# Two transformer-like layers on one core: hi and lo activations as one 512-column moving side in the wide products

## The chip, the cores and the metric

One core of a Trainium2 chip runs the whole program. The metric is device time in microseconds (us) of one execution, as the median of the runs; lower is better. Five engines work side by side, each through its own queue and in a fixed order: TensorE (PE, with its weight loads shown apart as PEld), VectorE (DVE), ScalarE (ACT), GpSimd (POOL) and SyncE (SP, which here only issues DMAs). TensorE writes to PSUM, which has eight banks of 512 f32 columns for each of 128 partitions.

## The reference

256 tokens of width 1024 pass through two layers, all in f32. Cut to what matters here:

```
first layer:   xn = rms_norm(x, norm1_g);  proj = xn @ w_in
               ... three small attentions on q, k, v -> o_nsa
               u = conv_c * conv_x;  y = 3-tap causal conv of u;  z = conv_b * y
               mixed = sigmoid(gate_a) * (o_nsa @ w_branch_a) + sigmoid(gate_b) * (z @ w_branch_b)
               x = x + mixed @ w_out
               x = x + square(relu(rms_norm(x) @ w_up)) @ w_down        # 1024 -> 4096 -> 1024
second layer:  a 31-tap convolution branch, an attention with top-k selection, two gates, their product with w_mix_out,
               cross attention to 256 memory rows (k, v = rms_norm(mem) @ wkv)
               h = h + square(relu(rms_norm(h) @ w_ff1)) @ w_ff2;  rms_norm(h)
```

conv_b, conv_c, conv_x, gate_a and gate_b are column ranges of proj, each 1024 wide.

## The kernel before

Activations are kept transposed: features on the 128 partitions, 256 tokens along the free side (T = 256). A weight matrix comes from HBM in units of 1 MB (`wr`, 128 x 2048: four blocks of 128 input features by 512 output features). Since f32 products are wanted from f32r passes, every number is split in two: ACT writes a rounded copy (`wh`, L123, two halves of 128x1024), DVE the rest (`wl`, L126, two halves). Activations are split in the same way into `hi` and `lo`. `Stream` loads and splits ahead: at the start of a unit it has the unit two further on split, and since there are three `wh`/`wl` buffers, that split has to wait until PE has left the unit just finished. So at every unit's start ACT's next `wh` half waits for PE.

A product of 128 input by 128 output features is `mm3` (L260 to L268): three matmuls of 256 moving columns into the same 256 PSUM columns, `wh` by hi (L264), `wh` by lo (L266) and `wl` by hi (L268). `Feat` is a group: 512 output features, so four such column ranges, in two PSUM tiles `m` of one bank each (a pool `psm` of four banks, so two groups have place at a time). A group takes `len(kts) // 4` units; most take two, the down products of the feed-forward eight. In its last unit a group goes through output features 0 and 1 first (called b = 0 below) and gives that tile to its eviction function while PE goes on with features 2 and 3 (b = 1). The eviction reads the PSUM tile itself: for instance `cs = ps * rb` (L802), `cs = ps * cs` (L805), `y = ps * y` (L820), `d = ps * rb` (L832), or `relu(ps)` on ACT (L929) followed by a square on DVE (L930) and the split into `hh` (L396 on ACT, L397 on DVE).

Between halves of a unit `pump()` runs one step of side work: the steps of the first layer's attentions, the statistics of the norms, the 31-tap convolution, the second attention. An attention step of the first layer has a few PE matmuls (scores L743 to L745, transposes L769, products L779 and L785), and on DVE a masked score (L747), a maximum (L750), reciprocals and scalings (L751 to L758). Ahead of these steps come two that go through POOL: `coqk` (L629 on DVE, L631 a power on POOL, L633 and on again on DVE) and `msc` (L688, L689 on POOL, `kcb` L694 on DVE).

PE's instructions keep the order in which they are written. ACT's and DVE's are ordered when the program is built, by a planner that knows priorities (side steps are urgent) and estimated times; on the chip each engine keeps that order, so an instruction that waits holds up all that stand behind it on its engine.

The order of the groups in the first layer: q, k, a token product (`Tok`), then for each half of the conv features (hf 0 and 1) conv_c, conv_x, conv_b; gate_a twice (`ta`), gate_b twice (`tb`), z by w_branch_b twice (`zs`), the attention branch, w_out, eight groups of w_up (the first two taken unit by unit in turn), two groups of w_down. Then the memory keys (`km`), and the second layer, whose feed-forward up product has eight groups again; its down product is a `Tok` product with 512 moving columns (L355 to L357).

Of the kernel before, what the change touches and what calls it, by code (L numbers as in the profile page):

```python
# [16 lines left out]
T = 256  # L17
# [38 lines left out]
class Split:  # L56
# [12 lines left out]
    def lo(self, k, n=1):  # L69
        return self._part(1, k, n)  # L70

    def _part(self, h, k, n):
# [88 lines left out]
def hybrid_conformer_kernel(ctx, tc, stop, dbg, xT, memT, wall, wtok, wkiwi, wcmp, par_d, cst_d, gfin_d, out):  # L161
# [5 lines left out]
    sm = ctx.enter_context(tc.tile_pool(name="sm", bufs=2))  # L167
    psm = ctx.enter_context(tc.tile_pool(name="psm", bufs=4, space=bass.MemoryType.PSUM))
    pss = ctx.enter_context(tc.tile_pool(name="pss", bufs=3, space=bass.MemoryType.PSUM))
# [22 lines left out]
    def PS(name="s"):  # L192
        return pss.tile([128, 512], F32, name=name, tag="s")

    def bc(ap, n):
# [19 lines left out]
    def v4(ap):  # L215
        return ap.rearrange("p n (s a) -> p n s a", s=2)
# [41 lines left out]
    ALL8 = list(range(8))  # L258

    def mm3(ps_ap, wh, wl, xh, xl, first, last, part=None):  # L260
        ps_ap = ps_ap.rearrange("p (a s) -> p a s", s=2)
        xh, xl = turns(xh), turns(xl)
        if part in (None, 0):
            P.matmul(out=ps_ap, lhsT=wh, rhs=xh, start=first, stop=False, skip_group_check=True)  # L264
        if part in (None, 1):
            P.matmul(out=ps_ap, lhsT=wh, rhs=xl, start=False, stop=False, skip_group_check=True)  # L266
        if part in (None, 2):
            P.matmul(out=ps_ap, lhsT=wl, rhs=xh, start=False, stop=last, skip_group_check=True)  # L268

    class Feat:  # L270


        def __init__(self, act, kts, evac, kmajor=False):
            self.act, self.kts, self.evac, self.kmajor = act, kts, evac, kmajor
            self.nch = len(kts) // 4
            self.ps = None

        def chunk(self, c):
            if self.ps is None:
                self.ps = [psm.tile([128, 2, T], F32, name="m", tag="m") for _ in range(2)]  # L280
            ps, act = self.ps, self.act
# [38 lines left out]
    class Tok:  # L320
# [10 lines left out]
        def chunks(self, c, num, mid=None):  # L331

            if self.ps is None:
                self.ps = [psm.tile([128, 512], F32, name="m", tag="m") for _ in range(2)]
            ps, act, n = self.ps, self.act, self.n
# [39 lines left out]
    def prod(gs, pair=False):  # L375
        if pair:
            for c in range(gs[0].nch):
                for g in gs:
                    g.chunk(c)
        else:  # L380
            for g in gs:
                for c in range(g.nch):
                    g.chunk(c)

    def group(act, kts, evac, kmajor=False):
        prod([Feat(act, kts, evac, kmajor)])

# [95 lines left out]
    with tc.manual_schedule(engines=MANUAL):  # L483
# [3 lines left out]
        with tc.manual_schedule(engines={mybir.EngineType.Activation}):  # L487
            nc.scalar.dma_start(out=par0, in_=par_d[:, 0:8])
            A.activation(out=S([128, 1], "tab"), in_=ones[:, 0:1], func=AF.Exp)
        warm = psm.tile([128, 2, T], F32, name="m", tag="m")  # L490
        for i in range(WARM):
# [306 lines left out]
        for hf in range(2):  # L798
# [23 lines left out]

            group(xs, ALL8, ev_c)
            group(xs, ALL8, ev_x)
            group(xs, ALL8, ev_b)

        ta, tb = B8(name="ta"), B8(name="tb")
        for dst in (ta, tb):
            for hf in range(2):
                def ev_g(ps, o, n):  # L830
                    d = dst[hf][:, o:o + n]
                    V.tensor_tensor(v4(d), ps, v4(bc(c1["rb"], n)), op=ALU.mult)  # L832
                    A.activation(out=d, in_=d, func=AF.Tanh, scale=0.5)

                group(xs, ALL8, ev_g)


        m1 = B8(name="m1")
        for hf in range(2):
            def ev_bb(ps, o, n):  # L840
                gated(m1[hf][:, o:o + n], tb[hf][:, o:o + n], ps)

            group(zs, ALL8, ev_bb)
        drain(at1)
# [12 lines left out]

        def residual(act, kts, x, sp, gname, scale_b=None, kmajor=False, pair=True, stats=None):

            def one(hf):  # L860
# [28 lines left out]

                return Feat(act, kts, ev, kmajor=kmajor and hf == 0)  # L890

# [6 lines left out]
        def ffn_up(act, src, tagr, bcast):  # L898
# [25 lines left out]
            for g in range(8):  # L924
                hs.tiles += HL("hh", 4).tiles

                def ev(ps, o, n, g=g):
                    r = S([128, 2, T], "pr", PR_BUFS)
                    A.activation(out=v4(r), in_=ps, func=AF.Relu)  # L929
                    V.tensor_tensor(r, r, r, op=ALU.mult)  # L930
                    split_into(hs, r, n, 4 * g + o)

                gs.append(Feat(act, ALL8, ev))
            prod(gs[:2], pair=True)
# [44 lines left out]
        st3 = {}  # L979
        residual(hs, list(range(32)), x, None, None, scale_b=res["b"], pair=False, stats=st3)  # L980
        drain(msd)
# [31 lines left out]

        group(mems, ALL8, ev_km)
        drain(n3)
# [13 lines left out]
        def heads_pv(pt, nb, v, h0, sp, tt, pool=None):  # L1029

            if pool is psm:
                po = psm.tile([128, 2, T], F32, name="m", tag="m").rearrange("p a t -> p (a t)")
            else:
                po = PS() if pool is pss else pso.tile([128, 512], F32, name="o", tag="o")
# [163 lines left out]
        for hf in range(2):  # L1198
# [21 lines left out]
            kiwi = S([128, T], "rb", 4)  # L1220
            ps = psm.tile([128, 2, T], F32, name="m", tag="m")
            wh, wl = W.next()
# [302 lines left out]
```

## Time and profile before

| | |
|---|---|
| runs, median (lowest to highest) | 895.32 us (895.29 to 895.41), 3 runs |
| profiled execution, its own time | 895.22 us |
| its span, first to last instruction | 893.4 us |
| PE busy | 881.9 us (99%), 7240 matmuls |
| DVE busy | 659.8 us (74%) |
| ACT busy | 545.4 us (61%) |
| POOL busy | 18.6 us (2%) |

Times inside the execution are microseconds from the span's start. A row of the timeline gives start, duration, engine, line, operation, out<-in, and in brackets the idle time of the engine before it and what ended that. Matmuls overlap in the pipeline, so the distance from one matmul's start to the next is what it costs, not its duration; DVE and ACT instructions overlap by about 0.1 us with the next.

### The profile page before, as it was taken

The numbers are of one execution on the slowest core, as the hardware profiler recorded it, in microseconds if no ns is written. First come the engines' busy times: TensorE is split into PE (matmuls) and PEld (weight loads), VectorE is DVE, ScalarE is ACT, GpSimd is POOL, SyncE is SP. The second block draws the span as 40 slices with busy tenths as digits, with TensorE's granted clock in tenths as the row PEclk, the third lists the DMA queues.
The fourth block names the chain that finished last, engine by engine and source line by source line (L and its number), as shares of the span: only waits on it lengthen the run. The fifth ranks groups of instructions, "written<-read, shape, count | busy, mean of one in ns | idle before, by whom it ended". The sixth has DMA issues, their size and how long they took to land.

```text
span 893.4 us, 17269 instructions
## 1 busy us (share of the span) xinstructions
PE 881.9 (99%) x7240; PEld 852.8 (95%) x7240; DVE 659.8 (74%) x1037; ACT 545.4 (61%) x925; POOL 18.6 (2%) x21
## 2 busy tenths in 40 slices
PE   9999999999999999999999999999999999999996
PEld 8999999999999999999998989999999999998885
DVE  6678899457787675648699999997787777665542
ACT  7634667444575564434697799977566657554432
POOL 0121000000000000000000000000000000000000
PEclk9999999999999999999999999999999999999999
DMA  8944623455555566554553356354565265555531
GB/s 305 313 161 146 222 98 140 158 211 198 190 190 189 192 241 219 197 189 140 186 209 107 139 193 236 112 192 166 199 250 203 104 216 189 190 202 209 198 142 48
DMA packets 25566, 165.01 MB, mean 185 GB/s; under 512 B 2960, under 2 KB 3600, under 8 KB 6928
## 3 DMA queue, kind: packets, MB, share of 16 engines
q1 hardware_dynamic: 25056, 163.37, 51.8%
q8 instruction: 57, 0.93, 0.4%
q10 hardware_dynamic: 432, 0.53, 0.2%
q14 instruction: 21, 0.17, 0.1%
HBM read 162.58 MB, written 1.05 MB: 183 GB/s over the span
## 4 chain that ended last, share of the span: by engine, by line
PE 89%; DVE 5%; ACT 2%; issue 1%; DMA 1%; POOL 1%; POOLq 0%; DVEq 0%
PE m L264 23%; PE m L266 23%; PE m L268 23%; PE m L355 4%; PE m L356 4%; PE m L357 4%; DVE wl L126 2%; PE m L295 2%; DMA wr<-in_wall_dram 1%; PE m L352 1%; DVE y L1147 1%; PE o L785 1%; PE s L769 1%; PE s L1065 1%; POOL coqk L631 1%
## 5 line engine op out<-in xcount | busy, mean ns | idle before, releaser
L126 DVE TENSOR_TENSOR wl<-wr,wh 128x1024 fp32r<-128x1024 f32 (+2 forms) x300 | 350.4, 1191 | 155.2 <-ACT wh L123 154.8
L123 ACT ACTIVATE wh<-wr 128x1024 fp32r<-128x1024 f32 (+2 forms) x300 | 298.5, 1028 | 204.2 <-PE m L266 95.9
L264 PE MATMUL m<-xnh,wh 128*128 128x256 f32 x376 | 106.6, 283 | 0.0
L266 PE MATMUL m<-xnh,wh 128*128 128x256 f32 x376 | 103.4, 275 | 0.0
L268 PE MATMUL m<-xnh,wl 128*128 128x256 f32 x376 | 103.4, 275 | 0.0
L264 PE MATMUL m<-xh,wh 128*128 128x256 f32 x384 | 100.5, 282 | 0.9 <-ACT xh L523 0.9
L266 PE MATMUL m<-xh,wh 128*128 128x256 f32 x384 | 98.0, 276 | 0.0
L268 PE MATMUL m<-xh,wl 128*128 128x256 f32 x384 | 97.8, 275 | 0.0
L1146 ACT ACTIVATE cp<-u,par 128x255 f32<-128x255 f32 (+23 forms) x192 | 78.8, 492 | 0.0
L266 PEld LDWEIGHTS m<-xnh,wh 128*128 128x128 f32 x376 | 72.2, 192 | 0.7 <-issue 0.5
L264 PEld LDWEIGHTS m<-xnh,wh 128*128 128x128 f32 x376 | 72.2, 192 | 0.7 <-issue 0.5
L264 PEld LDWEIGHTS m<-xh,wh 128*128 128x128 f32 x384 | 69.8, 192 | 2.8 <-issue 1.4
L268 PEld LDWEIGHTS m<-xnh,wl 128*128 128x128 f32 x376 | 72.2, 192 | 0.0
L264 PE MATMUL m<-x5h,wh 128*128 128x256 f32 x256 | 70.8, 277 | 0.0
L264 PE MATMUL m<-fh,wh 128*128 128x256 f32 x256 | 70.6, 276 | 0.0
L264 PE MATMUL m<-hh,wh 128*128 128x256 f32 x256 | 70.6, 276 | 0.0
L268 PE MATMUL m<-x5h,wl 128*128 128x256 f32 x256 | 70.4, 275 | 0.0
L266 PE MATMUL m<-fh,wh 128*128 128x256 f32 x256 | 70.4, 275 | 0.0
L268 PE MATMUL m<-fh,wl 128*128 128x256 f32 x256 | 70.4, 275 | 0.0
L266 PE MATMUL m<-hh,wh 128*128 128x256 f32 x256 | 70.4, 275 | 0.0
L268 PE MATMUL m<-hh,wl 128*128 128x256 f32 x256 | 70.4, 275 | 0.0
L266 PE MATMUL m<-x5h,wh 128*128 128x256 f32 x256 | 70.4, 275 | 0.0
(380 smaller groups left out, 2318.1 us busy)
## 6 DMA issues: line engine op xcount, KB each, us to landing
wr<-in_wall_dram SPq DMA_DIRECT2D x145, 1024.0 KB, 4.9
wr<-in_wall_dram SPq DMA_DIRECT2D x4, 512.0 KB, 9.1
mem<-in_memT_dram SPq DMA_DIRECT2D x4, 512.0 KB, 5.8
wr<-in_wtok_dram SPq DMA_DIRECT2D x2, 560.0 KB, 5.5
wr<-in_wall_dram SPq DMA_DIRECT2D x4, 256.0 KB, 5.1
wck<-in_wcmp_dram SPq DMA_DIRECT2D x2, 512.0 KB, 8.6
cst<-in_cst_dram SPq DMA_DIRECT2D x1, 776.0 KB, 10.7
x<-in_xT_dram SPq DMA_DIRECT2D x2, 256.0 KB, 4.2
```

The source lines that it names most:

```text
L123: self.nc.scalar.activation(out=hi[:, sl], in_=raw[:, sl], func=AF.Copy)
L126: self.nc.vector.tensor_sub(lo[:, sl], raw[:, sl], hi[:, sl].bitcast(F32))
L264: P.matmul(out=ps_ap, lhsT=wh, rhs=xh, start=first, stop=False, skip_group_check=True)
L266: P.matmul(out=ps_ap, lhsT=wh, rhs=xl, start=False, stop=False, skip_group_check=True)
L268: P.matmul(out=ps_ap, lhsT=wl, rhs=xh, start=False, stop=last, skip_group_check=True)
L295: P.matmul(out=plain(ps[o // 2])[:, o % 2], lhsT=wh[:, kk, sl], rhs=v3(act.raw(k)), start=first, stop=last, skip_group_check=True)
L352: P.matmul(out=o.rearrange("p a s -> p s a"), lhsT=act.raw(k)[:, tk], rhs=wh[:, w], start=first, stop=last)
L355: P.matmul(out=o, lhsT=xh, rhs=wh[:, w], start=first, stop=False)
L356: P.matmul(out=o, lhsT=xh, rhs=wl[:, w], start=False, stop=False)
L357: P.matmul(out=o, lhsT=xl, rhs=wh[:, w], start=False, stop=last)
L631: G.tensor_tensor(co, ms, mhalf, op=ALU.pow)
L1146: A.activation(out=p[:, i, 0:T - d], in_=u[hf][:, i, 0:T - d], func=AF.Copy, scale=w[i])
```

## The change

Products of certain groups are done by `mm2` in place of `mm3`: one matmul of `wh` by hi and lo side by side (512 moving columns) into a whole bank, and one of `wl` by hi (256 columns) into the bank's first half. A 128-feature output then takes a bank, and a group four banks: two tiles of the new pool form `PM` (two banks each, two of them, so the same four banks in all). The two halves of a bank are added at the eviction: ACT copies the second halves of two banks to an SBUF tile `pr`, DVE adds the first halves to it, and the old eviction function works on `pr` instead of PSUM. Inside a unit the order is b, then input block, then output, in every unit and not only in the last.

This holds for (`wide=True`) the six conv groups, the four gate groups, the two of z, groups 2 to 7 of both up products, the two w_down groups of the first layer and the memory keys: 25 groups of two units and two of eight, 66 units of 16 products, 1056 products. Where relu and square came as ACT and DVE instructions, wide up groups take `max(p, 0) * p` on DVE. All other groups keep `mm3` and take one `PM` tile.

```diff
+    def both(self, k):
+        return self.tiles[k // 2][:, :, k % 2]
...
-    psm = ctx.enter_context(tc.tile_pool(name="psm", bufs=4, space=bass.MemoryType.PSUM))
+    psm = ctx.enter_context(tc.tile_pool(name="psm", bufs=2, space=bass.MemoryType.PSUM))
...
+    def PM():
+
+        return psm.tile([128, 2, 2, T], F32, name="m", tag="m")
...
+    def mm2(ps_ap, wh, wl, xhl, first, last):
+
+        P.matmul(out=ps_ap.rearrange("p h (a s) -> p h a s", s=2), lhsT=wh, rhs=xhl.rearrange("p h (s a) -> p h a s", s=2),
+                 start=first, stop=False, skip_group_check=True)
+        P.matmul(out=ps_ap[:, 0].rearrange("p (a s) -> p a s", s=2), lhsT=wl, rhs=turns(xhl[:, 0]), start=False, stop=last,
+                 skip_group_check=True)
...
+        def chunk_wide(self, c):
+
+            if self.ps is None:
+                self.ps = [None, None]
+            wh, wl = (w.rearrange("p (k o) -> p k o", k=4) for w in W.next())
+            ks = self.kts[4 * c:4 * c + 4]
+            end = c == self.nch - 1
+            for b in range(2):
+                if c == 0:
+                    self.ps[b] = PM()
+                m = self.ps[b]
+                for kk in range(4):
+                    for o in range(2):
+                        sl = slice((2 * b + o) * 128, (2 * b + o) * 128 + 128)
+                        mm2(m[:, o], wh[:, kk, sl], wl[:, kk, sl], self.act.both(ks[kk]), c == 0 and kk == 0, end and kk == 3)
+                if end:
+                    t = S([128, 2, T], "pr", PR_BUFS)
+                    A.activation(out=v4(t), in_=plain(m[:, :, 1]), func=AF.Copy)
+                    V.tensor_tensor(v4(t), plain(m[:, :, 0]), v4(t), op=ALU.add)
+                    self.evac(v4(t), 2 * b, 2)
+                pump()
+
         def chunk(self, c):
+            if self.wide:
+                self.chunk_wide(c)
+                return
             if self.ps is None:
-                self.ps = [psm.tile([128, 2, T], F32, name="m", tag="m") for _ in range(2)]
+                m = PM()
+                self.ps = [m[:, 0], m[:, 1]]
...
-            group(xs, ALL8, ev_c)
-            group(xs, ALL8, ev_x)
-            group(xs, ALL8, ev_b)
+            group(xs, ALL8, ev_c, wide=True)
+            group(xs, ALL8, ev_x, wide=True)
+            group(xs, ALL8, ev_b, wide=True)
...
                 def ev(ps, o, n, g=g):
                     r = S([128, 2, T], "pr", PR_BUFS)
-                    A.activation(out=v4(r), in_=ps, func=AF.Relu)
-                    V.tensor_tensor(r, r, r, op=ALU.mult)
+                    if g < 2:
+                        A.activation(out=v4(r), in_=ps, func=AF.Relu)
+                        V.tensor_tensor(r, r, r, op=ALU.mult)
+                    else:
+                        V.scalar_tensor_tensor(out=v4(r), in0=ps, scalar=0.0, in1=ps, op0=ALU.max, op1=ALU.mult)
                     split_into(hs, r, n, 4 * g + o)

-                gs.append(Feat(act, ALL8, ev))
+                gs.append(Feat(act, ALL8, ev, wide=g > 1))
```

The change also moves instructions on ACT and DVE. Three places follow; lines of the changed kernel are other than those of before (copy L309, add L310, `wh` L126, `wl` L129).

Place 1, DVE, at the end of the first conv group (hf 0, conv_c, b = 0), in the kernel before:

```order
L126 TENSOR_TENSOR wl<-wr,wh 128x1024 [waits Activation_49]
L633 TENSOR_SCALAR coqk<-coqk,r_354 128x8 [waits Pool_49]
L635 TENSOR_SCALAR coqk<-coqk,r_354 128x4
L633 TENSOR_SCALAR coqk<-coqk,r_354 128x8
L635 TENSOR_SCALAR coqk<-coqk,r_354 128x4
L638 COPY sqkR<-coqk 128x256 [waits DVE_49] x2
L126 TENSOR_TENSOR wl<-wr,wh 128x1024 [waits DMAHW2_49,Activation_49]
L126 TENSOR_TENSOR wl<-wr,wh 128x1024 [waits Activation_49]
L731 TENSOR_TENSOR cs__1203<-coqk,cst 128x16
L802 TENSOR_TENSOR cs<-m,rb 128x512 [waits PE_49]
```

and in the changed kernel:

```order
L670 TENSOR_SCALAR msqk<-s,r1sq_357 128x12 [waits PE_49]
L674 TENSOR_SCALAR coqk<-coqk,r_352 128x8 [waits Pool_49]
L676 TENSOR_SCALAR coqk<-coqk,r_352 128x4
L674 TENSOR_SCALAR coqk<-coqk,r_352 128x8
L676 TENSOR_SCALAR coqk<-coqk,r_352 128x4
L679 COPY sqkR<-coqk 128x256 [waits DVE_49] x2
L772 TENSOR_TENSOR cs__1087<-coqk,cst 128x16
L129 TENSOR_TENSOR wl<-wr,wh 128x1024 [waits DMAHW2_49,Activation_49]
L129 TENSOR_TENSOR wl<-wr,wh 128x1024 [waits Activation_49]
L310 TENSOR_TENSOR pr<-m,pr 128x512 [waits Activation_49]
```

The add, the last reader of the PSUM tile, stands where L802 stood: behind the wait for POOL and two `wl` halves. The `wl` half that stood between `msqk` and the wait has moved ahead of `msqk`. PE's first matmul of conv_x now waits for this add.

Place 2, DVE, at the end of the first gate_a group (`ta`, hf 0), in the kernel before:

```order
L747 SCALAR_TENSOR_TENSOR pr<-s,cs__1203,cst 128x512 [waits PE_49]
L756 TENSOR_TENSOR mx<-mx,gate 128x2 [waits DVE_49]
L126 TENSOR_TENSOR wl<-wr,wh 128x1024
L758 TENSOR_SCALAR pr<-pr,mx 128x256 [waits DVE_49]
L758 TENSOR_SCALAR pr<-pr,mx 128x256
L750 TENSOR_REDUCE mx<-pr 128x2
L832 TENSOR_TENSOR ta<-m,rb 128x512
L751 TENSOR_SCALAR mx<-mx 128x2 [waits DVE_49]
L747 SCALAR_TENSOR_TENSOR pr<-s,cs__1203,cst 128x512 [waits PE_49]
```

and in the changed kernel:

```order
L788 SCALAR_TENSOR_TENSOR pr<-s,cs__1087,cst 128x512 [waits PE_49]
L792 TENSOR_SCALAR mx<-mx 128x2 [waits DVE_49]
L129 TENSOR_TENSOR wl<-wr,wh 128x1024
L791 TENSOR_REDUCE mx<-pr 128x2 [waits DVE_49]
L796 RECIPROCAL mx<-mx 128x2 [waits Activation_49]
L831 TENSOR_TENSOR oh<-o,oh 128x128 [waits Activation_49]
L797 TENSOR_TENSOR mx<-mx,gate 128x2 [waits DVE_49]
L792 TENSOR_SCALAR mx<-mx 128x2
L310 TENSOR_TENSOR pr<-m,pr 128x512
```

L788 is L747 of before, and it is the same one in both pieces that stands last above and first below (the twelfth of sixteen). The eviction of b = 0 stood ahead of it, and now stands behind it, a `wl` half and a reduction.

Place 3, ACT, from one up group of the feed-forward to the next, in the kernel before (L396 is the split of b = 0, L929 the relu of b = 1):

```order
L396 ACTIVATE hh<-pr 128x512 [waits DVE_49]
L123 ACTIVATE wh<-wr 128x1024 [waits DMAHW1_49,PE_49]
L929 ACTIVATE pr<-m 128x512 [waits PE_49]
L123 ACTIVATE wh<-wr 128x1024
L396 ACTIVATE hh<-pr 128x512 [waits DVE_49]
```

and in the changed kernel, where DVE's order is `wl`, add (L310), `wl`, `max(p, 0) * p`:

```order
L437 ACTIVATE hh<-pr 128x512 [waits DVE_49]
L126 ACTIVATE wh<-wr 128x1024 [waits DMAHW1_49,PE_49,Activation_49]
L309 ACTIVATE pr<-m 128x512 [waits PE_49,Activation_49]
L126 ACTIVATE wh<-wr 128x1024
L437 ACTIVATE hh<-pr 128x512 [waits DVE_49]
```

ACT's order is the same, with the copy in the relu's place. The tile was free after L929; now it is free after the add on DVE that follows the copy, and PE's next group needs it.

## Rows read from the trace of the kernel before

**Rows 1.** The page's first section: busy us (share) xinstructions by engine.

```profile
PE 881.9 (99%) x7240; PEld 852.8 (95%) x7240; DVE 659.8 (74%) x1037; ACT 545.4 (61%) x925; POOL 18.6 (2%) x21
```

**Rows 2.** Windows, a stretch of feed-forward: length, busy (xinstructions) of PE, PEld, DVE, ACT, POOL, clock.

```profile
250.00:300.00 50.00, 50.00 (x450) 50.00 (x449) 37.76 (x48) 31.96 (x43) 1.08 (x1) 1.00 0.55 191
```

**Rows 3.** Timeline of PE in the last product: first and last of 16 matmuls.

```profile
829.65 0.38 PE L356 MATMUL m<-wl,hh 128*128 128x512 f32 x1
...
832.89 0.38 PE L356 MATMUL m<-wl,hh 128*128 128x512 f32 x1
```

**Rows 4.** What PE waited for, longest first.

```profile
PE s L1164 <- DVE ys L1161: 1.1, 1, 1.1
```

**Rows 5.** Timeline of DVE, POOL and ACT around the end of the first conv group.

```profile
44.42 0.37 DVE L629 TENSOR_SCALAR msqk<-s,r1sq 128x12 f32<-128x12 f32 x2 [0.20 <-PE s L623]
...
49.98 0.23 DVE L633 TENSOR_SCALAR coqk<-coqk,r 128x8 f32<-128x8 f32 x1 [4.07 <-POOL coqk L631]
...
50.92 2.36 DVE L126 TENSOR_TENSOR wl<-wr,wh 128x1024 fp32r<-128x1024 f32 x2
...
53.28 0.69 DVE L802 TENSOR_TENSOR cs<-m,rb 128x512 f32<-128x512 f32 x1
...
44.93 5.02 POOL L631 TENSOR_TENSOR coqk<-msqk,mhalf 128x24 f32<-128x24 f32 x1 [18.79 <-DVE msqk L629]
...
49.77 2.02 ACT L123 ACTIVATE wh<-wr 128x1024 fp32r<-128x1024 f32 x2 [3.36 <-PE m L266]
```

**Rows 6.** Timeline of DVE behind that: a memset and eight small adds of the attention.

```profile
54.13 0.91 DVE L643 MEMSET Bkv<- 128x1024 f32 x1 [0.16 <-issue]
...
55.50 2.31 DVE L649 TENSOR_TENSOR Bkv<-kcvE,par 128x120 f32<-128x120 f32 x8
```

**Rows 7.** Timeline of POOL and DVE in the hf 0 conv_b group, which starts at 67.1.

```profile
69.98 3.81 POOL L689 TENSOR_TENSOR msc<-msc,mhalf 128x16 f32<-128x16 f32 x1 [20.03 <-DVE msc L688]
...
73.82 0.35 DVE L694 TENSOR_TENSOR kcb<-kcr,msc 64x16 f32<-64x16 f32 x2 [2.79 <-POOL msc L689]
```

**Rows 8.** Timeline of PE, ACT and DVE where one up group follows another.

```profile
285.96 0.28 PE L264 MATMUL m<-fh,wh 128*128 128x256 f32 x1
...
286.05 1.06 ACT L123 ACTIVATE wh<-wr 128x1024 fp32r<-128x1024 f32 x1 [0.58 <-PE m L266]
287.02 0.58 ACT L929 ACTIVATE pr<-m 128x512 f32<-128x512 f32 x1
...
287.15 1.23 DVE L126 TENSOR_TENSOR wl<-wr,wh 128x1024 fp32r<-128x1024 f32 x1 [0.95 <-ACT wh L123]
288.29 0.69 DVE L930 TENSOR_TENSOR pr<-pr 128x512 f32<-128x512 f32 x1
```

**Rows 9.** Windows of 10 us in the attention steps, same columns: first and last of three.

```profile
110.00:120.00 10.00, 10.00 (x96) 9.54 (x92) 9.95 (x31) 7.64 (x22) 0.00 (x0) 1.00 0.45 165
...
130.00:140.00 10.00, 10.00 (x88) 9.45 (x87) 10.00 (x23) 6.82 (x18) 0.00 (x0) 1.00 0.31 108
```

**Rows 10.** Timeline of PE and DVE at the end of the first gate_a group.

```profile
132.63 0.38 PE L745 MATMUL s<-kzh,ql 128*128 128x512 f32 x1
...
134.18 0.38 PE L264 MATMUL m<-xh,wh 128*128 128x256 f32 x1
...
134.40 0.77 DVE L747 SCALAR_TENSOR_TENSOR pr<-s,cs__1203,cst 128x512 f32<-128x512 f32 x1
...
135.66 0.70 DVE L750 TENSOR_REDUCE mx<-pr 128x2 f32<-128x512 f32 x1
```

**Rows 11.** Windows at the program's end, same columns; the clock stands after POOL.

```profile
886.00:888.00 2.00, 0.58 (x3) 0.18 (x1) 1.16 (x4) 0.86 (x4) 0.00 (x0) 1.00 0.40 154
888.00:890.00 2.00, 0.00 (x0) 0.00 (x0) 0.94 (x3) 0.77 (x2) 0.55 (x1) 0.96 0.00 0
890.00:893.00 3.00, 0.00 (x0) 0.00 (x0) 0.00 (x0) 0.00 (x0) 0.00 (x0) 0.50 0.45 175
```

**Rows 12.** Groups of instructions, all shapes apart: xcount, busy us, mean ns of one.

```profile
L864 DVE TENSOR_TENSOR x<-m,x 128x512 f32<-128x512 f32 x12 | 8.0, 686 | 4.4 <-PE m L268 4.4
...
L929 ACT ACTIVATE pr<-m 128x512 f32<-128x512 f32 x32 | 18.8, 587 | 9.5 <-PE m L268 9.5
```

More of the change, by code (lines that the diff above doesn't have):

```diff
@@ L270, in hybrid_conformer_kernel, with __init__ @@
     class Feat:
-        def __init__(self, act, kts, evac, kmajor=False):
-            self.act, self.kts, self.evac, self.kmajor = act, kts, evac, kmajor
+        def __init__(self, act, kts, evac, kmajor=False, wide=False):
+            self.act, self.kts, self.evac, self.kmajor, self.wide = act, kts, evac, kmajor, wide
             self.nch = len(kts) // 4
             self.ps = None
+        def chunk_wide(self, c):
[18 more added lines that the diff above has]
+                pump()
         def chunk(self, c):
+            if self.wide:
+                self.chunk_wide(c)
+                return
             if self.ps is None:
-                self.ps = [psm.tile([128, 2, T], F32, name="m", tag="m") for _ in range(2)]
+                m = PM()
+                self.ps = [m[:, 0], m[:, 1]]
             ps, act = self.ps, self.act
@@ L333, in chunks @@
             if self.ps is None:
-                self.ps = [psm.tile([128, 512], F32, name="m", tag="m") for _ in range(2)]
+                m = PM().rearrange("p b a t -> p b (a t)")
+                self.ps = [m[:, 0], m[:, 1]]
             ps, act, n = self.ps, self.act, self.n
@@ L383, in prod, with group @@
                     g.chunk(c)
-    def group(act, kts, evac, kmajor=False):
-        prod([Feat(act, kts, evac, kmajor)])
+    def group(act, kts, evac, kmajor=False, wide=False):
+        prod([Feat(act, kts, evac, kmajor, wide)])
     def tok_group(act, kts, n, evac):
@@ L489, in hybrid_conformer_kernel @@
             A.activation(out=S([128, 1], "tab"), in_=ones[:, 0:1], func=AF.Exp)
-        warm = psm.tile([128, 2, T], F32, name="m", tag="m")
+        warm = PM()[:, 0]
         for i in range(WARM):
@@ L833, in ev_g @@
                     A.activation(out=d, in_=d, func=AF.Tanh, scale=0.5)
-                group(xs, ALL8, ev_g)
+                group(xs, ALL8, ev_g, wide=True)
         m1 = B8(name="m1")
@@ L841, in ev_bb @@
                 gated(m1[hf][:, o:o + n], tb[hf][:, o:o + n], ps)
-            group(zs, ALL8, ev_bb)
+            group(zs, ALL8, ev_bb, wide=True)
         drain(at1)
@@ L856, in hybrid_conformer_kernel, with residual @@
         prod([ba(0), ba(1)])
-        def residual(act, kts, x, sp, gname, scale_b=None, kmajor=False, pair=True, stats=None):
+        def residual(act, kts, x, sp, gname, scale_b=None, kmajor=False, pair=True, stats=None, wide=False):
             def one(hf):
@@ L888, in ev @@
                         later.append((STATS_LAG, add_up))
-                return Feat(act, kts, ev, kmajor=kmajor and hf == 0)
+                return Feat(act, kts, ev, kmajor=kmajor and hf == 0, wide=wide)
             prod([one(0), one(1)], pair=pair)
@@ L979, in hybrid_conformer_kernel @@
         st3 = {}
-        residual(hs, list(range(32)), x, None, None, scale_b=res["b"], pair=False, stats=st3)
+        residual(hs, list(range(32)), x, None, None, scale_b=res["b"], pair=False, stats=st3, wide=True)
         drain(msd)
@@ L1012, in ev_km @@
             V.tensor_tensor(v4(km[:, o:o + n]), ps, v4(bc(rmb, n)), op=ALU.mult)
-        group(mems, ALL8, ev_km)
+        group(mems, ALL8, ev_km, wide=True)
         drain(n3)
@@ L1031, in heads_pv @@
             if pool is psm:
-                po = psm.tile([128, 2, T], F32, name="m", tag="m").rearrange("p a t -> p (a t)")
+                po = PM()[:, 0].rearrange("p a t -> p (a t)")
             else:
@@ L1220, in hybrid_conformer_kernel @@
             kiwi = S([128, T], "rb", 4)
-            ps = psm.tile([128, 2, T], F32, name="m", tag="m")
+            ps = PM()[:, 0]
             wh, wl = W.next()
```

## The prediction

> **What bounds the kernel now.** I read the page's busy shares first, then PE's waits, then windows. PE is busy 99% of the span [rows 1], its longest wait anywhere is 1.1 us [rows 4], and in the feed-forward 450 matmuls of 256 columns fill 50 us without a gap at clock 1.00 [rows 2]. So PE's stream of matmuls is the time, and the reader should see two things: what one matmul costs, and that nobody makes PE wait today. DVE (74%) and ACT (61%) are hidden, with one weak stretch: from 110 to 140 us DVE is busy 9.95 to 10 of every 10 us [rows 9], while PE still runs through. Any change on PE counts at once; any work put on DVE counts only where PE comes to wait for it.
>
> **What the change takes from PE.** 450 matmuls in 50 us are 111.1 ns each [rows 2]. A matmul of 512 columns costs (832.89 - 829.65) / 15 = 216.0 ns [rows 3]. So a product costs 3 x 111.1 = 333.3 ns before, and 216.0 + 111.1 = 327.1 ns after: the columns are the same, and what is saved is the start of one matmul, 6.2 ns. 1056 products give 6.5 us. No row shows a 512-column matmul followed by a 256-column one; the bounds are 0 (the pair costs what three cost) and 8.4 us (7.9 ns each, if the 256-column one too had only the 2.7 ns above its columns that the 512-column one has at 2.4 GHz).
>
> The rows put a 256-column matmul at 111.1 ns, 267 cycles of 2.4 GHz. The Trainium skill (TensorE: Matmul & The Clock Gate, "Back-to-back issue gap") lists 262 cycles for 256 columns and 518 for 512; by that page a product would save 6 cycles, an estimate of 2.6 us in all. The rows differ for 256 columns, and decide.
>
> **What it adds.** For each of 54 evictions DVE gets an add of 128x512 from PSUM, 0.69 us like L864, and ACT a copy of 0.59 us like L929 [rows 12]; 24 of the copies replace a relu. That work alone is hidden where DVE is at 74%. What is not hidden is the hand-over of PSUM. Before, a group left its two banks and the next took two others, so an eviction had a whole group's time. Now a wide group fills all four banks, so the next group's b = 0 waits for the add of b = 0, and its b = 1 for the add of b = 1. From the end of either half PE has only the other half in hand, 8 x 0.327 = 2.6 us plus the side step's matmuls, and the add stands in DVE's queue behind whatever the planner put ahead of it. Each term below is that wait.
>
> S1, hf 0 conv groups. Conv_c ends at about 49.7 (ACT's `wh` is released by PE at 49.77) [rows 5], 0.2 earlier with the gain. Conv_x's first matmul needs the add of b = 0, which stands in L802's place (place 1): behind a POOL power of 5.02 us that ends at 49.95, the `coqk` steps and two `wl` halves (2.36 us). L802 began at 53.28 [rows 5]. As one `wl` half now stands ahead of `msqk`, POOL starts up to 1.1 us later; I take 0.8. The add ends at 53.28 + 0.69 + 0.8 = 54.8, PE waits 54.8 - 49.5 = 5.3 us. Behind it on DVE come the old eviction (0.6), the memset (0.9), a `wl` half (1.2), the eight small adds (2.3) [rows 5, 6] and then the add of b = 1, done at about 60.2; PE wants it at 54.8 + 2.6 + 0.8 (a side step) = 58.2: 2.0 us. In conv_b the add of conv_x's b = 1 stands behind `kcb`, which waits for POOL's `msc`. DVE hands `msc` over late before (POOL starts 2.9 us into the group [rows 7]); with PE held up DVE is no longer late and it leaves some 0.6 us before the group starts. Then 0.25 + 3.81 + 0.35 [rows 7], a `wl` half of 1.14 and the add of 0.69: done 5.6 us into the group, wanted at 2.6: 3.0 us. S1 = 10.3 (8 to 12).
>
> S2, hf 1 conv and gates, where DVE is full. At the first gate group's end the add of b = 0 now stands behind the twelfth L747 and more (place 2). Its score leaves PE at 132.63 + 0.38; L747 starts at 134.40, and DVE has no earlier time for it, being full [rows 9, 10]. From its start: 0.66, 0.07, `wl` 1.14, the reduction 0.60, four small ones 0.45, the add 0.69, that is 3.6 us, so 138.0 on the old clock, while PE's next group wants to start at 134.18 [rows 10]: 3.8 us. The hand-over before it (conv_b to gate) I put at 1.0, since the add of b = 1 comes out some 0.5 to 2 us after PE wants it when the two adds ahead of it are counted; the two conv ones at 0.5 and 0.2. S2 = 5.5. Lower bound: only the added work that doesn't fit, eight adds of 0.6 less 2.3 us idle between 100 and 150 = 2.5; upper 7.
>
> S3, the regular hand-overs. Where one up group follows another [rows 8] the next starts at 285.96, so its b = 1 would start at 288.58. ACT first does `wh` (it waits for PE's last use of the buffer) and then the tile's eviction; DVE does `wl` until 288.38, and the next instruction, in whose place the add stands (place 3), starts at 288.29 and ends at 288.98. PE goes on at 289.03, 0.45 us late. This pattern stands in the order eight times between up groups (four in each layer; groups 2 to 3 have the copy and the add first and no wait): 3.6 us. The three between `tb` and `zs` groups 0.4 each, with the side step: 1.2. Three have more ahead of the add: groups 3 to 4 of the first layer (two `wl` halves) 1.3, the two w_down groups 0.5, w_down to the memory keys 1.1. S3 = 7.7; bounds 4 (if copies run ahead of `wh`) and 10.
>
> C, the clock. PE's last matmul ends at 886.6, the clock reads 0.96 in 888 to 890 and 0.50 after that [rows 11]: it fell to its lower level (1.2 GHz) some 3.3 us after PE stopped. No wait inside the kernel before comes near that; the first of S1 (5.3) does, and those of 3.0 and 3.8 may. While it is low PE does half. No row shows how long it stays low under work; I take one spell of the 3 us seen, 1.5 us lost; bounds 0 and 4.
>
> Sum: 895.2 (this execution; the median of the runs is 0.1 above it) - 6.5 + 10.3 + 5.5 + 7.7 + 1.5 = **913.7 us**, 2.1% slower. With all low ends it is 895.2 - 8.4 + 8 + 2.5 + 4 = 901.3, with all high ends 895.2 + 12 + 7 + 10 + 4 = 928.2.
>
> **The rivals.** A, the other side: the adds are done within 2.6 us. It needs ACT and DVE to take copy and add first; then only the gain is left, 895.2 - 6.5 = 888.7. It decides at every hand-over alike: below 2.6 us from PE's end to the add's end it wins. For it: the bare chain is 0.1 + 0.59 + 0.69 = 1.4 us. Against it: the order in places 1 to 3, which the chip keeps, and DVE's idle wait of 4.07 us for POOL at exactly the place where the first add now stands.
>
> B, waits but half of them: PE's first wait lets DVE and ACT run ahead, and the later ones of S1 and S2 shrink to their low ends or vanish: first wait 5.3, S2 2.5, S3 4, no clock term: 895.2 - 6.5 + 11.8 = 900.5. For it: DVE's backlog is what delays L802 and L805 before. Against: the wait for POOL and the `wh` that waits for PE don't depend on a backlog.
>
> D, the gain fails: a 512-column matmul over two pieces with hi and lo 512 elements apart, or its pairing with a short one, costs what two cost. Then 913.7 + 6.5 = 920.2. Against: the last product's 512-column matmuls also read pairs that lie apart and run at 216.0 ns.
>
> E, the clock falls again and again. There are 24 hand-overs from one wide group to the next, and if PE's pause in each cost a spell like C's, it is 24 x 1.5 = 36 instead of 1.5, so 948.2. Against: most waits are 0.45 us, and a wait of 1.1 us left the clock at 1.00. The Trainium skill (TensorE: Matmul & The Clock Gate, "A second HAM failure mode: psum-queue depth-cycling") tells of a kernel whose clock kept falling because PE paused briefly between matmul groups while PSUM was cycled. No row here shows that.
>
> **How the numbers follow.** Forecast (the sum, 904 to 919): 0.66. A: 0.06. B (896 to 904): 0.14. D and larger waits (919 to 925): 0.10. E: 0.04. Below a range from 900 to 921 lie A and the lower part of B, above it E and half of D, about 0.2 together, so that is the range. A measurement of this kernel can tell about 0.2% (1.8 us) from no change. Faster by more: A, 0.06. Within: the lowest part of B, 0.03. Slower by more: all else, 0.91.
>
> **What would show it.** PE's rows: 512- and 256-column starts 216 and 111 ns apart. PE's waits: m waiting for DVE pr (the add), about 20 of them, the longest near 50 us into the span with 5 us, two more of 3 to 4 us before 140, and eight of 0.4 to 0.5 between up groups. DVE busy grows by 54 x 0.69 = 37 us, ACT by 30 x 0.59 = 18 us. The clock should dip once after the longest wait. The forecast is wrong if PE's idle time stays under 10 us, if ACT's copy starts ahead of the `wh` half at the hand-overs, or if the pair costs other than 327 ns.

## The result, and the profile after

The changed kernel takes 996.76 us (median, 995.0 to 997.52), the kernel before 895.34: a ratio of 1.113, with a 95% interval from 1.1111 to 1.1149. The forecast was 913.7 with a range from 900 to 921. The direction was right, and four fifths of the loss were not in the sum.

The page of the kernel after: its span, busy time by engine, and the granted clock in 40 slices (tenths).

```profile
span 995.7 us, 15252 instructions
PE 909.1 (91%) x6184; PEld 839.2 (84%) x6184; DVE 697.6 (70%) x1091; ACT 562.8 (57%) x955; POOL 16.1 (2%) x21
PEclk9999998998999999997999999999999999999999
```

Two things stand beside [rows 1]: PE is idle for 995.7 - 909.1 = 86.6 us (11.5 before), and its mean clock is 0.974 (0.998 before). Its busy time has grown in spite of 1056 fewer matmuls, mostly because part of it ran at the lower clock.

**The gain came.** Timeline of PE in a wide up group: a matmul of 512 columns (L269) and one of 256 (L271) by turns.

```profile
329.76 0.38 PE L269 MATMUL m<-fh,wh 128*128 128x512 f32 x1
329.98 0.27 PE L271 MATMUL m<-fh,wl 128*128 128x256 f32 x1
330.08 0.38 PE L269 MATMUL m<-fh,wh 128*128 128x512 f32 x1
```

0.22 and 0.10 us, together 0.32 to 0.33 for a product: over the five pairs from 329.76 to 331.39 it is 0.326. That is close to the 327 ns of the sum; three matmuls took 333.

**The waits that were forecast came too.** First hand-over, conv_c to conv_x: POOL, DVE and PE (compare [rows 5]).

```profile
49.85 4.17 POOL L672 TENSOR_TENSOR coqk<-msqk,mhalf 128x24 f32<-128x24 f32 x1 [24.23 <-DVE msqk L670]
54.06 0.23 DVE L674 TENSOR_SCALAR coqk<-coqk,r 128x8 f32<-128x8 f32 x1 [4.35 <-POOL coqk L672]
...
55.08 2.35 DVE L129 TENSOR_TENSOR wl<-wr,wh 128x1024 fp32r<-128x1024 f32 x2
57.36 0.68 DVE L310 TENSOR_TENSOR pr<-m,pr 128x512 f32<-128x512 f32 x1
58.09 0.48 PE L269 MATMUL m<-xh,wh 128*128 128x512 f32 x1 [3.45 <-DVE pr L310]
```

From one up group to the next (compare [rows 8]): DVE's add, and PE's first matmul of the next group's b = 1.

```profile
335.50 0.68 DVE L310 TENSOR_TENSOR pr<-m,pr 128x512 f32<-128x512 f32 x1
336.24 0.48 PE L269 MATMUL m<-fh,wh 128*128 128x512 f32 x1 [0.42 <-DVE pr L310]
```

The add behind POOL and two `wl` halves makes PE wait 3.45 us (forecast 5.3), the regular hand-over 0.42 (forecast 0.45).

**What the forecast did not have.** PE's waits in the kernel after: PE's tile and line, releaser, us in all, times, longest.

```profile
PE m L269 <- DVE pr L310: 16.7, 16, 3.5
PE m L278 <- DVE x L905: 11.2, 5, 3.2
PE m L278 <- DVE u L228: 5.3, 2, 3.9
PE m L278 <- DVE ta L228: 5.1, 2, 2.7
...
PE m L278 <- ACT pr L971: 4.1, 4, 1.4
```

Only the first row belongs to the wide groups. L278 is the first matmul of `mm3`, so all the others shown are groups that "keep `mm3` and take one `PM` tile". Their releasers are evictions: the residual, the gated products, the relu. Two such places follow. First an ACT eviction (the second layer's q): PE's last matmul of b = 0, the eviction, PE's first of b = 1.

```profile
548.74 0.28 PE L282 MATMUL m<-xnh,wl 128*128 128x256 f32 x1
549.05 0.60 ACT L1277 ACTIVATE q<-m 128x512 f32<-128x512 f32 x1 [5.53 <-PE m L282]
549.70 0.38 PE L278 MATMUL m<-xnh,wh 128*128 128x256 f32 x1 [0.69 <-ACT q L1277]
```

Then a DVE eviction (attention branch, `ta`) with a `wl` half ahead of it, and the eviction that the wide group before it (`zs`) left to DVE (`m`).

```profile
219.79 0.28 PE L282 MATMUL m<-oh,wl 128*128 128x256 f32 x1
220.16 1.21 DVE L129 TENSOR_TENSOR wl<-wr,wh 128x1024 fp32r<-128x1024 f32 x1
221.29 0.75 DVE L228 SCALAR_TENSOR_TENSOR m<-tb,pr 128x256 f32<-128x256 f32 x2
221.96 0.74 DVE L228 SCALAR_TENSOR_TENSOR ta<-ta,m 128x256 f32<-128x256 f32 x2
222.76 0.38 PE L278 MATMUL m<-oh,wh 128*128 128x256 f32 x1 [2.69 <-DVE ta L228]
```

This is in the middle of a unit. b = 0 and b = 1 are different banks, but now one tile `m`, and the program makes PE wait to write a tile that an eviction still reads. Before, the two halves were two tiles, and PE went on with b = 1 at once: the list of its waits in the trace of before has no eviction of a group's `m`. There are 34 of these waits, 53.3 us: 29 at L278 and 5 in `Tok` groups. Each costs a little more than it shows: from 548.74 to 549.70 are 0.96 us, which is 0.11 for the matmul, 0.69 of idle time and 0.16 for stopping.

The second term is the clock. Windows before and behind the wait of 2.69 us, and behind that of 0.69: length, busy (xinstructions) of PE, PEld, DVE, ACT, POOL, then the clock.

```profile
218.00:223.00 5.00, 2.31 (x21) 2.12 (x20) 4.55 (x8) 1.81 (x3) 0.00 (x0) 1.00 0.44 152
223.00:228.00 5.00, 5.00 (x32) 5.00 (x32) 1.75 (x4) 1.33 (x2) 0.00 (x0) 0.66 0.48 195
549.70:553.00 3.30, 3.30 (x29) 3.30 (x30) 3.16 (x10) 3.30 (x9) 0.00 (x0) 1.00 0.88 288
```

PE works through the second window, but 32 matmuls pass where 45 would [rows 2]: it runs at 1.2 GHz for some 3.4 of the 5 us. Of the 14 waits of 2.2 us and more in this trace 12 have such a spell behind them, in two places begun before the wait's end; of those up to 1.98 us none has, unless a longer one stands right behind it.

The span by terms, from the idle times of all PE rows:

| term | forecast | trace of after |
|---|---|---|
| gain of 1056 products | -6.5 | -6.5 (taken as forecast) |
| hand-overs out of wide groups | +23.5 | +20.7 (S1 7.7; S2 3.4; S3 5.6; memory keys to the next group 4.0) |
| waits inside units of `mm3` groups | 0 | +53.3 |
| memory statistics, late | 0 | +3.8 |
| small waits of before that are gone | 0 | -2.7 |
| lower clock: 0.026 x 995.7 less 0.002 x 893.4 | +1.5 | +24.1 |
| stopping, 53 x 0.16 | 0 | +8.5 |
| sum on a span of 893.4 | 911.9 | 994.6 (measured 995.7) |

The terms are good to a few us and not to one. The clock term counts idle time inside a spell as lost, and behind a wait the second matmul too comes 0.1 us late (549.70 to 549.91 for 0.11), some 5 us in 53 waits, which the table leaves out.

### The profile page after: what moved, and what is told of

Its sections match the earlier page's. It is cut to its first block, busy times and chain, and to the rows that moved or that the text cites. A ratio compares the mean times of both kernels' runs of the same rounds, so it can differ in the third digit from the quotient of the medians.

```text
span 995.7 us, 15252 instructions
## 1 busy us (share of the span) xinstructions
PE 909.1 (91%) x6184; PEld 839.2 (84%) x6184; DVE 697.6 (70%) x1091; ACT 562.8 (57%) x955; POOL 16.1 (2%) x21
## 4 chain that ended last, share of the span: by engine, by line
PE 65%; DVE 19%; ACT 8%; issue 4%; DMA 2%; POOL 1%; POOLq 0%; ACTq 0%; DVEq 0%
PE m L269 18%; PE m L271 9%; DVE wl L129 9%; PE m L278 8%; PE m L280 7%; PE m L282 7%; ACT wh L126 4%; PE m L396 3%; PE m L397 3%; PE m L398 3%; PE m L335 2%; DMA wr<-in_wall_dram 1%; DVE pr L310 1%; ACT cp L1190 1%; DVE y L1191 1%
## 5 line engine op out<-in xcount | busy, mean ns | idle before, releaser
L129 DVE TENSOR_TENSOR wl<-wr,wh 128x1024 fp32r<-128x1024 f32 (+2 forms) x300 | 350.0, 1189 | 156.1 <-ACT wh L126 155.8
L126 ACT ACTIVATE wh<-wr 128x1024 fp32r<-128x1024 f32 (+2 forms) x300 | 298.8, 1027 | 228.6 <-issue 86.5
L278 PE MATMUL m<-xnh,wh 128*128 128x256 f32 x376 | 108.7, 289 | 18.9 <-DVE u L228 5.3
L269 PE MATMUL m<-xh,wh 128*128 128x512 f32 x320 | 112.6, 399 | 11.2 <-DVE pr L310 11.1
L278 PEld LDWEIGHTS m<-xnh,wh 128*128 128x128 f32 x376 | 73.5, 195 | 22.9 <-DVE u L228 6.3
L271 PE MATMUL m<-xh,wl 128*128 128x256 f32 x320 | 88.9, 278 | 0.0
L269 PE MATMUL m<-hh,wh 128*128 128x512 f32 x256 | 84.5, 383 | 0.7 <-DVE pr L310 0.7
L269 PEld LDWEIGHTS m<-xh,wh 128*128 128x128 f32 x320 | 62.2, 194 | 22.2 <-DVE pr L310 8.9
L271 PE MATMUL m<-hh,wl 128*128 128x256 f32 x256 | 69.8, 273 | 0.0
L269 PE MATMUL m<-fh,wh 128*128 128x512 f32 x192 | 63.8, 385 | 2.5 <-DVE pr L310 2.5
L1191 DVE TENSOR_TENSOR y<-y,cp 128x1020 f32<-128x1020 f32 (+23 forms) x48 | 55.6, 1158 | 14.5 <-ACT cp L1190 13.1
L269 PE MATMUL m<-x5h,wh 128*128 128x512 f32 x192 | 64.1, 386 | 1.7 <-DVE pr L310 1.7
L271 PEld LDWEIGHTS m<-xh,wl 128*128 128x128 f32 x320 | 63.1, 197 | 0.0
L269 PEld LDWEIGHTS m<-hh,wh 128*128 128x128 f32 x256 | 48.4, 189 | 7.9 <-DVE pr L310 1.3
L271 PE MATMUL m<-x5h,wl 128*128 128x256 f32 x192 | 52.3, 273 | 0.0
L271 PE MATMUL m<-fh,wl 128*128 128x256 f32 x192 | 52.3, 273 | 0.0
L396 PE MATMUL m<-wh,hh 128*128 128x512 f32 x128 | 48.7, 381 | 2.6 <-DVE x5t L1426 1.6
```

The costliest lines, as they stand in the source:

```text
L126: self.nc.scalar.activation(out=hi[:, sl], in_=raw[:, sl], func=AF.Copy)
L129: self.nc.vector.tensor_sub(lo[:, sl], raw[:, sl], hi[:, sl].bitcast(F32))
L269: P.matmul(out=ps_ap.rearrange("p h (a s) -> p h a s", s=2), lhsT=wh, rhs=xhl.rearrange("p h (s a) -> p h a s", s=2), start=first, stop=Fa ...
L271: P.matmul(out=ps_ap[:, 0].rearrange("p (a s) -> p a s", s=2), lhsT=wl, rhs=turns(xhl[:, 0]), start=False, stop=last, skip_group_check=True)
L396: P.matmul(out=o, lhsT=xh, rhs=wh[:, w], start=first, stop=False)
L1191: V.tensor_tensor(y[hf][:, :, d:T], y[hf][:, :, d:T], p[:, :, 0:T - d], op=ALU.add)
```

## The experiments

Theory T: the shared two-bank tile of the groups that stay at three matmuls is the loss, and behind its long waits the clock. Rival W: the wide products, through their longer evictions on ACT and DVE, delay everything. Rival K: the clock falls because of the 512-column matmuls or the hand-overs between wide groups.

**Bank tiles: undo the shared tile, keep all wide groups.**

```diff
-    psm = ctx.enter_context(tc.tile_pool(name="psm", bufs=2, space=bass.MemoryType.PSUM))
+    psm = ctx.enter_context(tc.tile_pool(name="psm", bufs=4, space=bass.MemoryType.PSUM))
...
-        return psm.tile([128, 2, 2, T], F32, name="m", tag="m")
+        return psm.tile([128, 2, T], F32, name="m", tag="m")
...
-                    self.ps[b] = PM()
+                    self.ps[b] = [PM() for _ in range(2)]
...
-                    A.activation(out=v4(t), in_=plain(m[:, :, 1]), func=AF.Copy)
-                    V.tensor_tensor(v4(t), plain(m[:, :, 0]), v4(t), op=ALU.add)
+                    for o in range(2):
+                        A.activation(out=v3(t[:, o]), in_=plain(m[o])[:, 1], func=AF.Copy)
+                    for o in range(2):
+                        V.tensor_tensor(v3(t[:, o]), plain(m[o])[:, 0], v3(t[:, o]), op=ALU.add)
...
-                m = PM()
-                self.ps = [m[:, 0], m[:, 1]]
+                self.ps = [PM() for _ in range(2)]
```

> The changed kernel with its PSUM tiles back at one bank each (four of them): a group that stays at three matmuls has two tiles again, a wide one takes two tiles for each half, and its copy and its add go bank by bank (two of 256 columns for one of 512). Theory T (the loss is the one two-bank tile of the groups that stayed at three matmuls: in the last unit PE may not write one bank while the eviction reads the other; 35 to 40 such waits in the trace of the changed kernel, about 58 us idle, and about 20 us more at the lower clock behind the long ones): those waits go, the hand-overs of the wide groups stay (16.7 us in the trace of the changed kernel) and the gain of 6.5 us too: 895 - 6.5 + 17 = 906, 900 to 912, granted clock 0.99 or more. Theory W (the wide products and their longer evictions on ACT and DVE delay everything): these stay, so over 970. Theory K (the clock falls because of the 512-column matmuls or the short pauses between wide groups): idle time falls but the clock stays near 0.974, so about 925.

917.37 us (915.0 to 918.92), ratio 1.0241 (1.0226 to 1.0256), clock 0.989. PE's longest waits, and the stretch of the up groups:

```profile
PE m L269 <- DVE pr L312: 11.3, 4, 4.5
PE m L278 <- DVE pr L312: 3.2, 1, 3.2
PE s L477 <- ACT pr L914: 3.1, 1, 3.1
```

```profile
300.00:350.00 50.00, 50.00 (x307) 46.01 (x306) 41.90 (x58) 31.65 (x48) 0.00 (x0) 1.00 0.60 214
```

The tiles alone give back 79 of the 101 us. All waits inside units are gone, with every wide product and all added ACT and DVE work still there: W falls as the main cause. The regular waits between up groups are gone too, in the stretch shown (PE busy 50.00 of 50 us) and elsewhere; I put that down to a bank being free after its own short add, which this run does not separate. So the 79 us hold some 6 of the hand-overs of wide groups, which fell from 20.7 to 14.5. What is left is few and long: conv_c to conv_x (4.03), 1.54 in the first conv_b and 4.46 behind the first gate group (place 2), 1.27 from up group 3 to 4 of the first layer, and the end of w_down with the memory keys. The run lies 5 us above the range, because I gave it no price for the clock behind those waits: 0.011 x 913.2 = 10 us, 8 more than before. With it the span adds up: 893.4 - 6.5 + 17.3 idle + 8.2 = 912.4, against 913.2.

**Late eviction: keep the shared tile, move one line.** In a group of three matmuls b = 0 is evicted after the matmuls of b = 1.

```diff
                 for b in range(2):
                     for kk in range(4):
                         for o in (2 * b, 2 * b + 1):
                             one(kk, o)
-                    self.evac(plain(ps[b]), 2 * b, 2)
                     if b == 0:
                         pump()
+                for b in range(2):
+                    self.evac(plain(ps[b]), 2 * b, 2)
```

> The changed kernel with one line moved: in a group that stays at three matmuls the eviction of outputs 0 and 1 is written after the matmuls of outputs 2 and 3, so nothing reads the two-bank tile while PE still writes it. Tiles, wide groups, copies and adds are as in the changed kernel. Theory T: the waits inside the last units go, 895 - 6.5 + 17 for the hand-overs of wide groups + up to 8 for evictions that now come 2.7 us later (two at once at a group's end) = 906 to 914, clock 0.98 or more. Theory W: over 970, since no work is taken away. Theory K: clock near 0.974 and about 925.

937.34 us (936.36 to 939.49), ratio 1.0470 (1.0455 to 1.0484), clock 0.986. PE's waits:

```profile
PE m L269 <- DVE pr L310: 15.7, 18, 3.4
...
PE m L397 <- ACT v L1283: 2.6, 2, 1.8
PE m L397 <- ACT gate L649: 2.5, 1, 2.5
PE m L397 <- DVE x5t L1427: 1.6, 1, 1.6
```

The waits inside units of `Feat` groups are gone, and 59 us with them. It is 23 us above my range, mostly for two reasons: L397 is `Tok`, whose evictions I had not moved (7.7 us in all, 5 waits), and the long waits at hand-overs and at the memory statistics each had a spell of low clock behind them (0.014 x 936.1 = 13 us, 11 more than before).

**The shared tile alone: no wide group at all.** `wide` is False everywhere; `PM` as in the changed kernel, evictions as before.

> The two-bank tiles alone: no group is wide, all have three matmuls and the evictions of before, but each group takes one tile of two banks. Theory T: 27 more groups now wait in their last unit, 13 of them with an ACT eviction (0.7 to 1.4 us each, about 13 in all), 14 with DVE evictions in a full stretch (1.4 to 4, about 31) and perhaps 15 more at the lower clock; the 17 of the hand-overs go and the gain of 6.5 too: 997 - 17 + 6.5 + 13 + 31 + 15 = 1045, 1015 to 1065. Theory W: no wide products, so 895 to 900. Theory K: clock 0.99 or more, idle time of 60 to 110 us.

1017.23 us (1015.59 and 1018.88), ratio 1.1359 (1.1338 to 1.1379), clock 0.973: slower than the changed kernel. The page's busy times, and PE's longest waits:

```profile
PE 916.9 (90%) x7240; PEld 875.2 (86%) x7240; DVE 667.4 (66%) x1037; ACT 549.6 (54%) x925; POOL 17.8 (2%) x21
```

```profile
PE m L278 <- ACT pr L971: 12.8, 16, 1.8
PE m L278 <- DVE x L905: 11.1, 5, 3.2
PE m L278 <- DVE cs L843: 7.4, 2, 6.0
...
PE m L278 <- DVE ta L228: 3.8, 2, 2.4
```

The instructions are as many as in [rows 1], and yet PE is idle for 97 us. So neither W nor K is needed: the tile costs 122 us by itself where all groups have it. The changed kernel was 20 us faster than this one; its wide groups take a tile for each half and have no such waits. The wide groups did lengthen some of the others: the two waits for `ta` are 5.1 us in the changed kernel and 3.8 here. The time came out 28 below mine, within the range, and mostly for the clock: it cost 0.027 x 1013.8 less 1.8 = 25.6 us, 1.5 more than in the changed kernel where I had 15 more. The twelve up groups that now wait too added 8.7 us (12.8 less the 4.1 of the changed kernel) where I had 13 for ACT evictions, the groups with DVE evictions 29 where I had 31.

**The price of a wait, in the kernel before.** In up groups 2 to 7 of both layers, after b = 0 of the last unit, ACT copies the tile to SBUF, then n more times from SBUF to SBUF, and a one-column matmul of PE reads the last copy. n = 0 (short) and n = 4 (long).

```diff
+                    if b == 0 and self.dose:
+                        z = S([128, 2, T], "pr", PR_BUFS)
+                        A.activation(out=v4(z), in_=plain(ps[0]), func=AF.Copy)
+                        for _ in range(4):
+                            z2 = S([128, 2, T], "pr", PR_BUFS)
+                            A.activation(out=z2, in_=z, func=AF.Copy)
+                            z = z2
+                        P.matmul(out=PS()[:, 0:1], lhsT=ident, rhs=z[:, 0, 0:1], start=True, stop=True)
                     self.evac(plain(ps[b]), 2 * b, 2)
...
+                gs[-1].dose = g > 1
```

> The kernel before, with a wait of PE's put into groups 2 to 7 of both up products (12 places): after the matmuls of outputs 0 and 1 of the last unit ACT copies their PSUM tile to SBUF, and a one-column matmul of PE reads that copy before PE goes on. Nothing else is changed. PE waits 0.1 + 0.59 and up to 1.1 more where a wh half stands ahead on ACT: 0.7 to 1.8 us each, 8 to 21 us in all. Theory C1 (waits of 2.2 us and more bring the clock down behind them, those below 2 don't, as in the trace of the changed kernel): clock 0.995 or more, 895.3 + idle time + 2 for the drains = 906 to 919. Theory C2 (any pause of PE costs clock): clock 0.98, 12 x 1.7 = 20 more, 926 to 939.

911.42 us (910.84 to 912.79), ratio 1.0178 (1.0164 to 1.0191), clock 0.998.

> The same 12 places with four more copies from SBUF to SBUF in ACT's chain (four times 0.5 to 0.6 us): PE waits 2.8 to 4.2 us each, 34 to 50 in all. Theory C1: each wait is followed by some 3.4 us at the lower clock, 1.7 lost: 12 x 1.7 = 20 on top of the idle time, clock 0.975 to 0.98, 895.3 + 42 + 20 + 2 = 959, 949 to 970. Theory C3 (the lower clock in the changed kernel comes from its 512-column matmuls or its two-bank tiles and not from the waits): clock 0.995 or more, 931 to 948.

964.32 us (962.07 to 970.58), ratio 1.0786 (1.0749 to 1.0823), clock 0.974. The waits of the short dose (a group's sum, times, longest), and a window of 4 us behind one of them:

```profile
PE s L323 <- ACT pr L318: 9.3, 12, 1.7
```

```profile
262.45:266.45 4.00, 4.00 (x35) 4.00 (x36) 2.50 (x4) 1.98 (x3) 0.00 (x0) 1.00 0.42 115
```

The same of the long dose, with windows behind two of the waits:

```profile
PE s L323 <- ACT pr L321: 41.1, 12, 4.4
```

```profile
264.90:268.90 4.00, 4.00 (x23) 4.00 (x24) 1.38 (x2) 1.07 (x2) 0.00 (x0) 0.64 0.59 240
...
298.14:302.14 4.00, 4.00 (x35) 4.00 (x36) 1.39 (x2) 1.98 (x3) 0.00 (x0) 1.00 0.37 158
```

There is no wide product and no shared tile here. Twelve waits of 0.69 to 1.73 us leave the clock at 1.00 and cost 16 us, 1.3 each; 9.3 of the 16 are idle time, the rest are the added matmuls and the stops. So not every pause of PE costs clock: C2 falls. Twelve of 3.34 to 4.38 cost 69, of which 41 are idle time and 0.026 x 961.1 less 1.8 = 23 the clock. C1 holds and C3 falls: a long pause brings the clock down with no wide product and no shared tile. But not every time: eleven of the twelve waits are of the same 3.34 us, and three of these were followed by full clock, like the one at 298.14.

**Wide only where no wide group follows.** Bank tiles, and wide in up groups 3, 5 and 7 of both layers and the first w_down group: 320 products.

> One-bank tiles as in e1, and wide only where no wide group follows a wide one: up groups 3, 5 and 7 of both feed-forwards and the first w_down group of the first layer (20 units, 320 products, 2.0 us of gain by 6.2 ns each). A group of three matmuls that follows needs only the two banks of b = 0, evicted 2.6 us before the wide group ends; the next wide one finds b = 1 evicted long ago. Theory T with my account of the hand-over: no waits over 0.2 us, so 895.3 - 2.0 = 893.3, 892.8 to 895. If the extra copy and add hold PE up anyway: 895 to 899.

892.81 us (892.49 to 893.42), ratio 0.9971 (0.9959 to 0.9983), clock 0.999: by 0.3% faster than the kernel before, little but clear of the noise (before: 894.89 to 896.35). PE waits nowhere longer than 1.1 us, and no wait is for an add.

```profile
PE 879.3 (99%) x6920; PEld 841.5 (94%) x6920; DVE 669.4 (75%) x1065; ACT 546.6 (61%) x941; POOL 17.8 (2%) x21
```

320 matmuls fewer and 2.6 us less of PE busy [rows 1], where 2.0 were expected.

**Wide wherever the bank tiles' trace had no wait.** Bank tiles; wide in gate_b, z, up groups 3 to 7 of both layers and the first w_down group: 576 products.

> One-bank tiles as in e1, wide in the groups whose hand-overs made no wait in e1's trace: both gate_b groups, both of z, up groups 3 to 7 of both layers, the first w_down group; the conv groups, gate_a, up group 2, the second w_down group and the memory keys stay at three matmuls. 36 units of 16 products, 576 x 6.2 ns = 3.6 us of gain. Theory T with copies and adds bank by bank: no wait over 0.3 us at hand-overs, 895.4 - 3.6 = 891.8, 891.2 to 893. If wide groups one behind the other still wait (0.4 us at ten places): 895.5.

892.74 us (891.88 to 893.46), ratio 0.9967 (0.9954 to 0.9979): faster than before by as little, within the range, and not to be told from the last one. The choice had a slip: the hand-over from up group 3 to 4 of the first layer had cost 1.27 us in the bank tiles' trace. It costs 1.21 here, where no wait over 0.3 was expected; two `wl` halves (2.45 us) and a split (0.68) stand ahead of the adds. With its stop it takes most of the 1.6 us by which the gain is larger:

```profile
278.64 0.45 PE L269 MATMUL m<-fh,wh 128*128 128x512 f32 x1 [1.21 <-DVE pr L312]
```

A wide group of two units gains 32 x 6.2 ns = 0.2 us. One wait of 1.2 us eats six of them.

## Why the prediction was wrong

**The gain (G)** was right: 0.326 us a pair measured, 0.327 forecast, and the kernel without hand-over waits (320 products) gained 2.6 us where its products give 2.0. Rival D falls.

**The hand-overs (S1 to S3)** were right in kind and mostly in place. In size 20.7 stands near the 23.5 forecast, but partly by luck: at the forecast places it was 16.7, and 4.0 came at the hand-over out of the memory keys, which the forecast did not have. S1 was 3.45, 1.89 and 2.40 where I had 5.3, 2.0 and 3.0. My 5.3 took both engines' times from the trace of before; in the trace of after PE came to this point 5 us later (58.09 - 3.45 = 54.64), held up at 38 us by a wait of 3.62 inside a `Tok` unit with a spell behind it, and POOL's step took 4.17 instead of 5.02. S2 was 3.4 where I had 5.5: the one at `ta` is the chain of place 2 (3.36, forecast 3.8), and the three others with 1.7 in sum did not come. S3 was 5.6 where I had 7.7: eight regular waits came, at 0.39 to 0.43, seven where I had them; the eighth was from up group 2 to 3 of the second layer, where I had none, and from 3 to 4 there was none.

**The failed step is in "What it adds": the hand-over of PSUM is priced for wide groups alone, and the last sentence on the change stands in the sum at nothing:** "All other groups keep `mm3` and take one `PM` tile." I counted banks (four for two groups, as before) and not tiles. The prediction itself priced the hand-over of PSUM by the rule that PE's next matmul waits for the last reader of its tile, and applied it to wide groups alone. For the others the same rule holds between b = 0 and b = 1, with at most a side step's matmuls between them, so that nearly every microsecond of the eviction counts. It could be priced from rows of before: [rows 8] has the relu that starts behind a `wh` half and takes 0.58, [rows 12] the residual's 0.69 for one add. 34 such places at 0.25 to 3.9 us are 53.3 us, and 9 of the 12 spells of lower clock lie at them. None of the forecast's three signs of being wrong looked at these groups: PE's idle time was over 10 us, a pair took 0.326 us, and between up groups the `wh` half still stood ahead of ACT's copy (333.29 and 334.23).

The Trainium skill (PSUM — Partial Sum Buffer, "Summary: rules for kernel authors") says to read a bank other than the one that matmuls write, and to guard by bank. The bank tiles agree: PE writes one bank while DVE and ACT read another, without a wait. So the lost time was not a need of the memory but of the tile by which the program counted it.

**The clock (C)** was mis-sized: 1.5 forecast with 4 as its upper bound, 24.1 measured, in 12 spells of about 2 us lost each. The price of one spell was near (1.5 against 2.0). The count was wrong: I had three long waits and the kernel has 14 of 2.2 us and more, and I read "some 3.3 us" from the program's end [rows 11], while in five places a wait of 2.2 to 2.7 us had a spell behind it. Rival E (948.2) was nearest in size, but not in cause: it charged every hand-over between wide groups, and of those only the long one at 149 us had a spell. The one dip that I forecast, behind the first wait of S1, did not come: there the clock stayed at 1.00. Of the other spells nine lie at waits inside `mm3` units, one at the memory statistics and one behind the memory keys. The Trainium skill (TensorE: Matmul & The Clock Gate, "A second HAM failure mode: psum-queue depth-cycling") tells of brief pauses that keep bringing the clock down. The traces agree for pauses of 2.2 us and more, 12 of 14 in the kernel after; they do not for the pauses of 0.4 to 0.7 us, which left it at 1.00.

Rival A falls: the hand-overs cost 16.7 us at the places where it has nothing. Rival B is off in time by far, but its mechanism is not refuted: 16.7 lies between its 11.8 and the forecast's 23.5, three of the four waits of S2 vanished, and those of S1 did not.

## What to carry to other kernels

When a change regroups on-chip memory, count what each user waits for in units of the program's own tracking (tiles), not of the hardware's (banks), and do it for the users that the change leaves alone too. Where PE is 99% busy and a change saves 0.2 us a group, one wait of 0.4 us a group already loses; apply it only where the evicted banks are not wanted next. Price a long wait of PE above its length: here those of 2.2 to 4.4 us mostly cost some 2 to 2.6 us of clock more, those up to 1.7 none.

## What was not expected of the hardware

The lower clock behind a pause is not a matter of the pause's length alone. In the kernel after, the wait of 3.45 us at 58.09 was followed by clock 1.00 and that of 2.20 at 259.65 by a spell; in the late eviction's trace the same wait of 3.45 us from conv_c to conv_x had a spell behind it. With the long dose the same 3.34 us had one in eight places and none in three. With the shared tile alone a wait of 1.85 us had a spell behind it and one of 2.42 none. What decides between them stays open.

A pause also costs more than the idle time shown. That is counted from the end of the last matmul, which is shown 0.28 us long though the next one would follow after 0.11; this is the 0.16 of the table.
